# Conformer convolution in a decoder trunk: the order in which eight normed tiles go through ScalarE and VectorE

## The chip, the cores and the metric

The kernel runs on one core of one Trainium2 chip. The metric is the time of one execution on the device in microseconds; of the kernel before there are three runs, and their median stands for it. One more execution was taken with the hardware profiler, and all durations of single instructions come from that one. The engines are called by the names of the profile: PE is TensorE, which multiplies matrices (PEld is its loading of weights), DVE is VectorE, ACT is ScalarE, POOL is GpSimd, SP is SyncE, whose queue issues most transfers.

## What is computed

The reference is a trunk of two layers on 512 tokens of width 1024 in float32. Each layer is a gated feed-forward part (`ffn1`), a mixer, a second one (`ffn2`) and a gated embedding (`ple`). The mixer of layer 0 is a Conformer convolution, that of layer 1 is sparse attention. The change lies in the convolution; cut to what matters:

```python
def conformer_conv(h, w_pw1, b_pw1, w_dw, b_dw, ln_g, ln_b, w_pw2, b_pw2):
    u = h @ w_pw1 + b_pw1
    a, g = jnp.split(u, 2, axis=-1)
    u = a * jax.nn.sigmoid(g)
    u = depthwise_causal_conv(u, w_dw) + b_dw            # 31 taps
    mu = jnp.mean(u, axis=-1, keepdims=True)
    var = jnp.mean(jnp.square(u - mu), axis=-1, keepdims=True)
    u = (u - mu) * lax.rsqrt(var + LN_EPS) * ln_g + ln_b
    u = jax.nn.silu(u)
    return u @ w_pw2 + b_pw2
```

## The kernel before

Activations lie transposed: eight tiles of 128 channels by 512 tokens. To keep float32 precision every product is made of three matmuls (`mm3`): each operand is split into a rounded high part `h` and a low part `l = x - h`, and the product is `wh*h` (L420), `wh*l` (L421) and `wl*h` (L422), summed in a PSUM bank. Weights arrive by DMA as units of 128 x 1024 (`raw`), are rounded on ACT (L334, `wh`), and their low part is made on DVE or POOL (L338, `wl`); for `conv_w_pw2` it is POOL. Five such pairs of buffers are there (`HLB`), so a unit can be rounded when the unit five before it has been used up. There are eight PSUM banks.

The convolution's last part goes as follows. When the depthwise filter's eight outputs `Y[c]` are there, with a first guess of the mean already taken off, PE forms the rest of the mean (`off`, in a bank) and the token sums; from these come the inverse deviation `r` (POOL, L501) and, by PE transposes (L526), the tile `R` of it, which stays in a PSUM bank. Meanwhile PE goes through the rest of the `fill`: products of the `ple` input (`z_tiles`, operands `zp`), one bank for each tile; ACT evicts each bank into a tile `t` (L762) and SP stores it to `z` in memory (L763). This fill covers the time in which the norm is worked out.

Then, for each of the eight tiles:

```python
nc.vector.tensor_tensor(Y[c], Y[c], off, op=OP.subtract)                  # L1038, DVE
nc.vector.tensor_tensor(Y[c], Y[c], R, op=OP.mult)                        # L1039, DVE
nc.scalar.activation(Y[c], Y[c], AF.Silu, scale=ln_g, bias=ln_b)          # L1040, ACT
nc.scalar.activation(h, Y[c], AF.Copy)                                    # L1041, ACT: rounding
nc.vector.tensor_tensor(l, Y[c], h.bitcast(F32), op=OP.subtract)          # L1042, DVE: low part
```

`h` and `l` are halves of a tile called `tw` (the buffers held the filter's taps before). They are the moving operands of the product with `conv_w_pw2`: for the first four output tiles PE goes tile by tile (`k` outside, four outputs `m` inside, 12 matmuls a tile), then for the other four output by output; 192 matmuls in all.

The text of the program doesn't fix the order in which an engine runs its instructions. A planner does so when the program is built (`schedule_with_timeline_sim=True`): it goes through a simulated time and gives each engine, of the instructions that are ready, the one of highest priority, which is the one that comes first in the text. `tc.high_priority(FIN_PRI)` raises the priority of a block. `tc.issue_after(x)` puts the block's instructions behind `x` where they are on the same engine. The order so found is then fixed, each engine runs its list in that order, and semaphores hold an instruction whose operands aren't there yet.

Of the kernel before, what the change touches and what calls it, by code (L numbers as in the profile page):

```python
# [11 lines left out]
F32 = mybir.dt.float32  # L12
F32R = mybir.dt.float32r
I32 = mybir.dt.int32
AF = mybir.ActivationFunctionType
OP = mybir.AluOpType
# [13 lines left out]
FIN_PRI = 100  # L30
CALM = ("ple_w_gate", "conv_w_pw2")
FIN_AT = (1, 3)
LATE, OUT_POOL, OUT_AMID = 3, ((), (1, 3, 6)), 3
PH, LAGS = 4, 9
CONV_ON = ("pool", "dve", "dve", "pe", "pe", "pe", "pe", "pe")
# [31 lines left out]
def plan():  # L67
# [87 lines left out]
    for i in range(L):  # L155
        ffn(1, i)
        if i == 0:
            conv(0)
        else:
            nsa()  # L160
        ffn(2, i)
        full("ple_w_gate", i, KD, range(KD))
# [50 lines left out]
class Kern:  # L213
# [726 lines left out]
    def conv(self, nxt):  # L940

        nc = self.nc
        X, U, Y = self.X, {}, []
# [86 lines left out]
        R = self.spread_raw(r)  # L1030
        for _ in fill:
            pass
        V = []
        for c in range(KD):
            pair = self.ptile("tw", TWB, 128 * LAGS, F32R)
            h, l = pair[:, :512], pair[:, 512:1024]
            with self.tc.issue_after(ui if c < CENTRED else vi):
                nc.vector.tensor_tensor(Y[c], Y[c], off, op=OP.subtract)  # L1038
            nc.vector.tensor_tensor(Y[c], Y[c], R, op=OP.mult)  # L1039
            nc.scalar.activation(Y[c], Y[c], AF.Silu, scale=self.col("conv_ln_g", c), bias=self.col("conv_ln_b", c))  # L1040
            nc.scalar.activation(h, Y[c], AF.Copy)  # L1041
            nc.vector.tensor_tensor(l, Y[c], h.bitcast(F32), op=OP.subtract)  # L1042
            V.append((h, l))
        self.prep_start(*nxt)
        for ms in (range(0, 4), range(4, 8)):
            P = {m: self.bank() for m in ms}
            for k, m in [(k, m) for k in range(KD) for m in ms] if ms[0] == 0 else [(k, m) for m in ms for k in range(KD)]:
                self.mm3(P[m], self.block(("conv_w_pw2", 0, k, m)), V[k], k == 0, k == KD - 1)
                if k == KD - 1:
# [86 lines left out]
    def put_v(self, g):  # L1136
        nc, t = self.nc, self.vt
        p = self.bank()
        for kt in range(4):
            nc.tensor.transpose(p[:, kt * 128:kt * 128 + 128], t[:, kt * 128:kt * 128 + 128], self.ident)  # L1140
        V = self.Vs[g % 2]
        p8 = p.rearrange("p (i d) -> p i d", d=64)
        nc.scalar.activation(V[:, :, :64], p8, AF.Copy)
        nc.vector.tensor_tensor(V[:, :, 64:], p8, V[:, :, :64].bitcast(F32), op=OP.subtract)

# [519 lines left out]
```

## Time and profile before

| | |
|---|---|
| median of three runs | 1967.86 us (1967.64 to 1968.73) |
| the profiled execution | 1969.18 us |
| its span | 1967.4 us, 32520 instructions |
| busy: PE, DVE, ACT, POOL | 1949.2, 1539.0, 1091.4, 328.8 us |
| the eight tiles' instructions in the span | L1038 from 490.7 us, L1042 until 512.4 us |
| the 192 matmuls of `conv_w_pw2` | 500.4 to 544.3 us |

In the profile a line such as "500.41 0.69 DVE L1042 ... x1" has the start in us from the span's start, the duration, the engine and line, the operation, output and inputs with their shapes, and how many equal instructions are merged. Behind it in brackets stands how long the engine had been idle and what released it. Matmuls overlap: one starts before the one ahead has ended, so start to start is their cost.

### The profile page before, as it was taken

How to read it: one execution, taken by the hardware profiler on the slowest of the kernel's cores; microseconds unless marked ns; L12 is line 12 of the kernel's file. 1: busy time of each engine (PE TensorE's matmuls, PEld its weight loads, DVE VectorE, ACT ScalarE, POOL GpSimd, SP SyncE). 2: the span in 40 equal slices, each digit the busy share in tenths (PEclk: the TensorE clock that was granted, in tenths of full speed). 3: DMA queues.
4: the chain of work that ended last, by engine and by line, in shares of the span. 5: the costliest groups of instructions: out<-in, count | busy, mean ns of one | idle time of the engine just before them, and what ended most of it. 6: DMA issues, size and time to landing. Idle time of an engine off the chain costs nothing.

```text
span 1967.4 us, 32520 instructions
## 1 busy us (share of the span) xinstructions
PE 1949.2 (99%) x12456; PEld 1752.0 (89%) x12456; DVE 1539.0 (78%) x2708; ACT 1091.4 (55%) x1958; POOL 328.8 (17%) x362
## 2 busy tenths in 40 slices
PE   9999999999999999999999999999999999999998
PEld 7989898889889898988999989888888789998987
DVE  7879787694697796877987868636889897786875
ACT  7536356653565363546644626337888765363543
POOL 0000000442200000021000000557666300000022
PEclk9999999999999999999999999999999999999999
DMA  5323323466335343343232423463323123232241
GB/s 174 129 86 110 127 87 103 178 216 222 114 118 162 96 158 112 100 150 107 85 132 85 134 82 101 154 193 108 96 87 102 44 97 119 97 119 97 97 150 54
DMA packets 79627, 235.16 MB, mean 120 GB/s; under 512 B 8864, under 2 KB 16176, under 8 KB 79472
## 3 DMA queue, kind: packets, MB, share of 16 engines
q1 hardware_dynamic: 78512, 230.69, 35.6%
q8 instruction: 98, 1.61, 0.3%
q0 software_dynamic: 816, 2.33, 0.3%
q14 instruction: 57, 0.47, 0.1%
q10 hardware_dynamic: 144, 0.07, 0.0%
HBM read 214.66 MB, written 16.29 MB: 117 GB/s over the span
## 4 chain that ended last, share of the span: by engine, by line
PE 93%; DVE 4%; ACT 2%; issue 1%; DMA 1%; SPq 0%; POOL 0%; POOLq 0%; DVEq 0%; ACTq 0%
PE b L420 28%; PE b L421 28%; PE b L422 28%; PE b L930 2%; PE b L1289 1%; PE b L1356 1%; PE b L1375 1%; PE b L1376 1%; PE b L1228 1%; PE b L520 0%; DVE t L1359 0%; DVE s L478 0%; DMA s<-in_xT 0%; ACT s L477 0%; DVE acc L495 0%
## 5 line engine op out<-in xcount | busy, mean ns | idle before, releaser
L420 PE MATMUL b<-s,wh 128*128 128x256 f32 (+1 forms) x1416 | 445.3, 317 | 2.2 <-ACT wh L334 2.1
L421 PE MATMUL b<-s,wh 128*128 128x256 f32 (+1 forms) x1416 | 445.2, 315 | 0.5 <-DVE s L478 0.3
L422 PE MATMUL b<-s,wl 128*128 128x256 f32 (+1 forms) x1416 | 443.3, 315 | 0.0
L334 ACT ACTIVATE wh<-raw 128x1024 fp32r<-128x1024 f32 (+2 forms) x254 | 266.1, 1050 | 232.0 <-PE b L421 134.6
L420 PE MATMUL b<-px,wh 128*128 128x256 f32 (+1 forms) x1088 | 312.6, 288 | 0.5 <-ACT G L578 0.5
L421 PE MATMUL b<-px,wh 128*128 128x256 f32 (+1 forms) x1088 | 312.9, 288 | 0.0
L422 PE MATMUL b<-px,wl 128*128 128x256 f32 (+1 forms) x1088 | 312.1, 288 | 0.0
L338 DVE TENSOR_TENSOR wl<-raw,wh 128x1024 fp32r<-128x1024 f32 (+1 forms) x208 | 253.8, 1222 | 61.7 <-ACT wh L334 61.3
L420 PEld LDWEIGHTS b<-s,wh 128*128 128x128 f32 x1416 | 266.0, 188 | 21.8 <-ACT wh L334 2.7
L421 PEld LDWEIGHTS b<-s,wh 128*128 128x128 f32 x1416 | 266.0, 188 | 19.2 <-DVE s L478 0.8
L422 PEld LDWEIGHTS b<-s,wl 128*128 128x128 f32 x1416 | 264.7, 188 | 19.1 <-DVE wl L338 0.5
L421 PE MATMUL b<-hid,wh 128*128 128x512 f32 x704 | 272.7, 389 | 0.0
L422 PE MATMUL b<-hid,wl 128*128 128x512 f32 x704 | 272.6, 389 | 0.0
L420 PE MATMUL b<-hid,wh 128*128 128x512 f32 x704 | 269.4, 389 | 0.0
L338 POOL TENSOR_TENSOR wl<-raw,wh 128x1024 fp32r<-128x1024 f32 (+1 forms) x53 | 129.2, 2444 | 691.7 <-ACT wh L334 686.5
L578 ACT ACTIVATE G<-b 128x256 f32<-128x256 f32 x390 | 140.6, 378 | 130.3 <-PE b L422 104.7
L420 PEld LDWEIGHTS b<-px,wh 128*128 128x128 f32 x1088 | 204.5, 188 | 5.5 <-ACT G L578 0.8
L421 PEld LDWEIGHTS b<-px,wh 128*128 128x128 f32 x1088 | 204.8, 188 | 4.3
L422 PEld LDWEIGHTS b<-px,wl 128*128 128x128 f32 x1088 | 204.5, 188 | 3.9
L422 PEld LDWEIGHTS b<-hid,wl 128*128 128x128 f32 x704 | 132.2, 188 | 27.1
L421 PEld LDWEIGHTS b<-hid,wh 128*128 128x128 f32 x704 | 132.2, 188 | 26.9
L420 PEld LDWEIGHTS b<-hid,wh 128*128 128x128 f32 x704 | 132.2, 188 | 26.9
(251 smaller groups left out, 3582.6 us busy)
## 6 DMA issues: line engine op xcount, KB each, us to landing
raw<-in_w SPq DMA_DIRECT2D x256, 512.0 KB, 3.3
rawx<-in_w SPq DMA_DIRECT2D x78, 512.0 KB, 3.3
tw<-in_tw SPq DMA_DIRECT2D x20, 576.0 KB, 6.5
skew<-table SPq DMA_DIRECT2D x16, 320.0 KB, 5.7
z<-t SPq DMA_DIRECT2D x16, 256.0 KB, 2.6
hid<-z SPq DMA_DIRECT2D x16, 256.0 KB, 4.4
tt<-skew SPq DMA_DIRECT2D x16, 256.0 KB, 3.3
wr<-in_w SPq DMA_DIRECT2D x8, 512.0 KB, 3.6
```

The lines of the kernel that those rows point to most:

```text
L334: self.rounded = nc.scalar.activation(h[:, c], t[:, c], AF.Copy).ins
L338: eng.tensor_tensor(l[:, c], t[:, c], h[:, c].bitcast(F32), op=OP.subtract)
L420: mm(out, sh, mh, start=start, stop=False, **how)
L421: mm(out, sh, ml, start=False, stop=False, **how)
L422: self.lastmm = mm(out, sl, mh, start=False, stop=stop, **how).ins
L578: copy = lambda o, x: nc.scalar.activation(o, x, AF.Copy)
L930: nc.tensor.matmul(p[:, q * SP:q * SP + SP], T[q][:, d * 128:d * 128 + 128], u[:, q, o:o + SP], start=d == 0, stop=d == LAGS - 1)
L1228: nc.tensor.matmul(P[mh][:, :124], w, B[kk // 4][:, kk % 4, :], start=kk == 0, stop=kk == 15)
L1289: nc.tensor.matmul(p[:, :32 - lo + nk], Q, KT[:, i, "sw".index(b), lo:32 + nk], start=i == 0, stop=i == 1)
L1356: nc.tensor.transpose(p[:, a * 128:a * 128 + 128], J[a, b][:, kt * 128:kt * 128 + 128], self.ident)
L1375: nc.tensor.matmul(O, st, h, start=first, stop=False)
L1376: nc.tensor.matmul(O, st, l, start=False, stop=last)
```

## The change

The subtraction stays as it is. The first three tiles (`AHEAD`) get high priority for the four instructions behind it. On ACT each Silu goes behind the rounding of the tile before, so that the activations go tile by tile; on DVE the multiplication of tile `c`, from the fourth on, goes behind the low part of tile `c - 3`.

```diff
+AHEAD = 3
...
-        V = []
+        V, high, low = [], [], []
         for c in range(KD):
             pair = self.ptile("tw", TWB, 128 * LAGS, F32R)
             h, l = pair[:, :512], pair[:, 512:1024]
             with self.tc.issue_after(ui if c < CENTRED else vi):
                 nc.vector.tensor_tensor(Y[c], Y[c], off, op=OP.subtract)
-            nc.vector.tensor_tensor(Y[c], Y[c], R, op=OP.mult)
-            nc.scalar.activation(Y[c], Y[c], AF.Silu, scale=self.col("conv_ln_g", c), bias=self.col("conv_ln_b", c))
-            nc.scalar.activation(h, Y[c], AF.Copy)
-            nc.vector.tensor_tensor(l, Y[c], h.bitcast(F32), op=OP.subtract)
+            with self.tc.high_priority(FIN_PRI) if c < AHEAD else nullcontext():
+                with self.tc.issue_after(low[c - AHEAD]) if c >= AHEAD else nullcontext():
+                    nc.vector.tensor_tensor(Y[c], Y[c], R, op=OP.mult)
+                with self.tc.issue_after(high[c - 1]) if c else nullcontext():
+                    nc.scalar.activation(Y[c], Y[c], AF.Silu, scale=self.col("conv_ln_g", c), bias=self.col("conv_ln_b", c))
+                high.append(nc.scalar.activation(h, Y[c], AF.Copy).ins)
+                low.append(nc.vector.tensor_tensor(l, Y[c], h.bitcast(F32), op=OP.subtract).ins)
             V.append((h, l))
```

## The prediction

> **What bounds the kernel now.** I read the page first, then the windows by stage, then the waits of the stretch that the change touches, and then that stretch instruction by instruction on each engine.
>
> ```profile
> span 1967.4 us, 32520 instructions
> ...
> PE 1949.2 (99%) x12456; PEld 1752.0 (89%) x12456; DVE 1539.0 (78%) x2708; ACT 1091.4 (55%) x1958; POOL 328.8 (17%) x362
> ...
> PE 93%; DVE 4%; ACT 2%; issue 1%; DMA 1%; SPq 0%; POOL 0%; POOLq 0%; DVEq 0%; ACTq 0%
> ```
>
> TensorE (PE) is busy for 1949.2 of 1967.4 us. All that any reordering of other engines' work can win is in the 18.2 us in which it isn't. The windows say where these lie (columns: length, then busy time and instructions of PE, PEld, DVE, ACT, POOL, then the granted clock, the DMA share and GB/s):
>
> ```profile
> core 0: us, PE busy (x) PEld busy (x) DVE busy (x) ACT busy (x) POOL busy (x), PEclk, DMA share, GB/s
> 495.00:500.00 5.00, 4.35 (x21) 3.27 (x18) 5.00 (x10) 3.77 (x7) 1.80 (x1) 1.00 0.74 239
> 500.00:545.00 45.00, 44.57 (x194) 36.17 (x195) 27.79 (x34) 23.28 (x35) 10.15 (x5) 1.00 0.26 89
> ...
> 545.00:750.00 205.00, 205.00 (x1498) 192.52 (x1497) 171.81 (x247) 113.66 (x183) 1.41 (x1) 1.00 0.41 133
> 750.00:970.00 220.00, 220.00 (x1335) 196.10 (x1334) 174.62 (x252) 113.61 (x174) 21.34 (x9) 1.00 0.32 107
> ...
> 1250.00:1620.00 370.00, 364.23 (x1991) 307.90 (x1991) 285.29 (x946) 259.86 (x703) 197.79 (x272) 1.00 0.34 107
> ```
>
> In the convolution's last part, 495 to 545, PE lacks 0.65 + 0.43 = 1.08 us. From 545 to 970 it lacks nothing, and attention (1250 to 1620) lacks 5.77. The waits from 495 to 520 name what the 1.08 us is:
>
> ```profile
> DVE tw L1042 <- ACT tw L1041: 4.4, 4, 2.0
> PEld b L420 <- ACT tw L1041: 1.5, 1, 1.5
> ...
> PE b L420 <- ACT tw L1041: 1.1, 1, 1.1
> ```
>
> PE waits here once, for the first rounded tile (L1041 writes `tw`). Its timeline shows the place, between the last matmul of the ple fill and the first of `conv_w_pw2`:
>
> ```profile
> 498.96 0.39 PE L422 MATMUL b<-zp,wl 128*128 128x512 f32 x1
> 500.43 0.96 PE L420 MATMUL b<-tw,wh 128*128 128x512 f32 x3 [1.08 <-ACT tw L1041]
> ```
>
> The matmuls that follow, and their operand tiles' own instructions, from the views by tile and by line:
>
> ```profile
> L420 PE MATMUL b<-tw,wh x64: 389/389/499, 500.4 to 543.4; 128*128 128x512 f32 x64
> L422 PE MATMUL b<-tw,wl x64: 388/389/395, 501.7 to 543.9; 128*128 128x512 f32 x64
> ...
> L1040 ACT ACTIVATE y<-y,small x8: 802/804/808, 497.2 to 505.6; 128x512 f32<-128x512 f32 x8
> L1041 ACT ACTIVATE tw<-y x8: 617/619/624, 499.8 to 509.3; 128x512 fp32r<-128x512 f32 x8
> L1042 DVE TENSOR_TENSOR tw<-y,tw x8: 685/692/2468, 500.4 to 510.0; 128x512 fp32r<-128x512 f32 x8
> ```
>
> The 192 matmuls start from 500.43 to 543.9: one per 43.47 / 191 = 0.2276 us. Without a wait the first would have started one step behind 498.96, at 499.19. So the wait costs 500.43 - 499.19 = **1.24 us** of PE time, and that is all this stage has to give. Why the first tile is late stands in the timelines of ACT and DVE:
>
> ```profile
> 494.22 1.22 ACT L762 ACTIVATE t<-b 128x512 f32<-128x512 f32 x2
> 496.67 0.60 ACT L762 ACTIVATE t<-b 128x512 f32<-128x512 f32 x1 [1.23 <-PE b L422]
> 497.16 2.21 ACT L1040 ACTIVATE y<-y,small 128x512 f32<-128x512 f32 x3
> 499.28 0.57 ACT L762 ACTIVATE t<-b 128x512 f32<-128x512 f32 x1
> 499.76 0.62 ACT L1041 ACTIVATE tw<-y 128x512 fp32r<-128x512 f32 x1
> ...
> 501.50 1.05 ACT L334 ACTIVATE wh<-raw 128x1024 fp32r<-128x1024 f32 x1
> ...
> 503.16 0.58 ACT L762 ACTIVATE t<-b 128x512 f32<-128x512 f32 x1
> ...
> 506.28 2.19 ACT L1041 ACTIVATE tw<-y 128x512 fp32r<-128x512 f32 x4
> ```
>
> ```profile
> 495.52 4.87 DVE L1039 TENSOR_TENSOR y<-y,b 128x512 f32<-128x512 f32 x8
> 500.41 0.69 DVE L1042 TENSOR_TENSOR tw<-y,tw 128x512 fp32r<-128x512 f32 x1
> ...
> 504.29 1.30 DVE L1042 TENSOR_TENSOR tw<-y,tw 128x512 fp32r<-128x512 f32 x1 [1.96 <-ACT tw L1041]
> ...
> 509.96 2.47 DVE L1042 TENSOR_TENSOR tw<-y,tw 128x512 fp32r<-128x512 f32 x1 [0.53 <-ACT tw L1041]
> ```
>
> ACT runs three Silus (2.21 us) and an eviction (0.57 us) before the one rounding that PE waits for; DVE runs eight multiplications (4.87 us) before the first low part.
>
> **The change part by part.** No instruction is added or removed, and no DMA: eight multiplications, Silus, roundings and low parts stay, in another order. The subtractions (L1038) stay ahead.
>
> *The first rounding.* Multiplication 0 starts at 495.52 and takes 0.68 (4.87 less seven steps of 0.60), to 496.20. Early case: Silu 0 follows at once, 496.24 to 497.04. Late case: it stays behind the eviction of 496.67 and starts at 497.16 as now, to 497.96. Then the rounding, at once. A Silu followed by an instruction that reads its tile is not in this trace on ACT. Below, it costs nothing over the overlap of free neighbours (three Silus in 2.21: a step of 0.70, overlap 0.10). Above, it costs what this pair costs on DVE, a running sum that reads its own result:
>
> ```profile
> 479.77 1.49 DVE L917 TENSOR_TENSOR sum<-sum,t 128x512 f32<-128x512 f32 x2 [2.23 <-ACT t L916]
> ```
>
> 1.49 less the second's 0.69 is a step of 0.80, against 0.60 in L1039: 0.20 more. I take 0.15, nearer the upper end, since the row has the same dependence. So the Silu's step is 0.70 to 0.90, I say 0.85, and rounding 0 ends at 497.7 early, 498.65 late. Both are before 499.19. The first matmul then needs nothing more: **-1.24 us**. At the lower edge, the late case plus a low part (0.03 behind the rounding, 0.69 long) gives 499.37, 0.18 late only if the second matmul is the one with the low part; today matmuls of the high part alone (L420) go first, as the row of 500.43 shows. I keep 0 to 0.2 as a loss, and take 0.
>
> *The other tiles.* One tile on ACT now takes 0.85 + 0.52 (rounding's step: 2.19 for four) = 1.37, up to 0.90 + 0.62 = 1.52; I take 1.45. DVE needs 0.60 + 0.69 = 1.29 a tile, less than ACT, so low part c - 3 is normally done before multiplication c is due. PE takes 12 matmuls a tile, 12 x 0.2276 = 2.73. Tile k is wanted at 499.19 + 2.73 k: 501.92, 504.65 ... 518.30. It is there, late case, at 498.65 + 1.45 k plus what ACT has beside: two evictions (0.57, 0.58) and one L334 (1.05), 2.2 together. Tile 1: 500.10, or 501.72 with an eviction and the L334 ahead: fits by 0.2. Tile 7: 508.8 + 2.2 = 511.0: fits by 7. Cost **0**; the cover is PE's slower pace.
>
> *What is pushed back.* High priority for three tiles puts up to 3 x 1.45 = 4.35 us of ACT work ahead of evictions and of the weight rounding L334. That L334 (501.50) rounds the fifth unit of `conv_w_pw2`, wanted when 96 matmuls are done, at 499.19 + 21.85 = 521.0; even at 505, with its low part on POOL, it is 13 us early. The evictions free PSUM banks (rivals) and feed `z`, which only the ple stage behind the second ffn reads. SP issues the `z` stores and the weight loads in one queue; a later eviction holds the next load, and the next unit has the same 13 us. POOL and its queue keep their instructions. Cost **0**.
>
> *Two SBUF readers.* The low parts of 504.29 and 509.96 took 1.30 and 2.47 where the median is 0.692, while POOL ran:
>
> ```profile
> 502.63 2.41 POOL L338 TENSOR_TENSOR wl<-raw,wh 128x1024 fp32r<-128x1024 f32 x1 [5.83 <-ACT wh L334]
> 509.48 2.39 POOL L338 TENSOR_TENSOR wl<-raw,wh 128x1024 fp32r<-128x1024 f32 x1 [4.44 <-ACT wh L334]
> ```
>
> They ended at 505.59 and 512.43, each 0.55 behind POOL's end (505.04, 511.87). A low part that meets an L338 on POOL so waits for its end, up to 2.47 - 0.69 = 1.78. After the change the next multiplications wait behind it. POOL's L338 needs the L334 before it, and that needs the buffer which the fill frees at 499.19, so POOL starts at 500.3 at the earliest. Low part 0 (498.65 at the latest) is clear; low part 2 or later has room; low part 1 is the one in question (rivals). In the sum: 0. [...]
>
> *Sum.* The profiled execution took 1969.18 us around a span of 1967.4, 1.32 over the median of 1967.86 (runs from 1967.64 to 1968.73). 1969.18 - 1.24 = 1967.94; on the median 1967.86 - 1.24 = **1966.6 us**, -0.06%. A difference of about 0.2% (3.9 us) is what a measurement of this kernel can tell from none.
>
> **The rivals.**
>
> *Nothing is gained.* The planner, which fixes each engine's order when the program is built, keeps the last fill tile's eviction ahead of rounding 0. That eviction can't start before PE's 498.96 + 0.39 = 499.35, so the rounding would end at 499.35 + 0.57 + 0.62 = 500.5: 500.43 again. For it: such an eviction stands there today (499.28). Against: high priority, and Silu 0 is ready three us before. 1967.9.
>
> *An eviction comes too late (slower).* Eight banks: at 499.19 four outputs, R (held until multiplication 7) and the last three fill tiles make exactly eight. If the fourth output gets the bank of the tile evicted at 496.67 and that eviction goes behind three tiles' chain, it ends at 496.24 + 4.35 + 0.6 = 501.2 to 497.16 + 4.35 + 0.6 = 502.1. The fourth output's first matmul is due at 499.19 + 3 x 0.2276 = 499.87: PE waits 1.3 to 2.2, net 0.1 to 1.0 slower: 1968.4. It decides from an end of 501.1 on. Against: two banks were freed by 495.44 (row of 494.22), the subtraction's `off` by 495.5, the sums' bank before.
>
> *Low part 1 meets POOL.* With an eviction and the L334 ahead, low part 1 starts near 500.7, just behind an L338 that ends about 503.0, and ends at 503.5. With four high-part matmuls first, PE wants it at 501.92 + 4 x 0.2276 = 502.83: 0.7 lost, 1967.3.
>
> *The planner orders later stages anew.* Priorities and a simulated time decide the order, and the simulated time moves. Attention holds 5.77 us of PE waits: all gone is 1960.8, doubled is 1972.4. Against: 425 us without a PE gap (545 to 970) lie between, and a common shift changes no order.
>
> **How the numbers follow.** Forecast 0.57, nothing gained 0.11, late bank 0.06, low part 1 0.05, new order later 0.21 (0.07 faster by over 0.2%, 0.08 slower, 0.06 within). Same: 0.57 + 0.11 + 0.06 + 0.05 + 0.06 = 0.85; faster 0.07; slower 0.08. The forecast alone would be 1966.1 to 1967.3 (0.2 lost, runs' scatter). The range goes up to the late bank's end, 1967.86 + 1.0 = 1968.9, and down by a third of attention's 5.77: 1966.6 - 1.9 = 1964.7.
>
> **What would show it.** ACT's timeline alternating L1040 and L1041 forms from 496.2 or 497.2, the first rounding done before 498.7; PE's first `tw` matmul 0.23 behind the last `zp` one and no wait for `tw`; DVE with three multiplications ahead of the first low part; the windows from 545 on the same, 1.2 earlier. I am wrong if PE waits there for an eviction, a low part or the same rounding, or if attention's 5.77 changes by more than 1.

## The result: slower by half a per cent, and the profile after

The changed kernel takes 1978.3 us (median of six runs, 1977.02 to 1979.4), the kernel before beside it 1968.01 (1967.64 to 1968.73): a ratio of 1.0051 with a 95% interval of 1.0038 to 1.0064. The forecast of 1966.6 and its range up to 1968.9 were missed by some 10 us, on the slow side. The profiled execution took 1978.41 us around a span of 1976.6, against 1969.18 and 1967.4 before. Lines of the changed kernel stand one further down than before, from the convolution's tiles on up to four.

The page and the windows of the changed kernel, the latter in the columns shown before:

```profile
span 1976.6 us, 32527 instructions
...
PE 1951.7 (99%) x12456; PEld 1754.4 (89%) x12456; DVE 1541.3 (78%) x2708; ACT 1093.0 (55%) x1958; POOL 339.4 (17%) x362
...
PE 90%; DVE 5%; ACT 2%; DMA 1%; issue 1%; POOL 1%; SPq 0%; POOLq 0%; DVEq 0%; ACTq 0%
```

```profile
495.00:500.00 5.00, 5.00 (x25) 3.99 (x23) 3.22 (x7) 3.71 (x7) 1.90 (x1) 1.00 0.78 237
500.00:545.00 45.00, 45.00 (x198) 36.32 (x197) 31.10 (x37) 25.06 (x37) 10.15 (x5) 1.00 0.28 91
545.00:750.00 205.00, 197.60 (x1438) 185.53 (x1437) 165.28 (x237) 109.22 (x177) 12.18 (x1) 0.98 0.39 125
...
970.00:1000.00 30.00, 28.69 (x250) 28.29 (x248) 28.83 (x44) 18.38 (x32) 0.00 (x0) 1.00 0.28 91
...
1250.00:1620.00 370.00, 364.06 (x1951) 306.15 (x1950) 285.71 (x940) 257.87 (x699) 203.69 (x278) 1.00 0.35 111
```

Where the change was made, PE now lacks nothing: 5.00 of 5.00 and 45.00 of 45.00. Attention lacks 5.94 us, as good as the 5.77 before. But 545 to 750, where PE had been busy throughout, lacks 7.40 us and has a granted clock of 0.98, and POOL, with one instruction there as before, is busy for 12.18 us instead of 1.41. That is the beginning of `ffn2` of layer 0. The view of L502, the inverse root formed as a power on POOL (below "the power"), has the same instruction:

```profile
L502 POOL TENSOR_TENSOR r<-v,power x9: 695/1027/12177, 355.1 to 1968.3; 128x4 f32<-128x4 f32 x7, 128x2 f32<-128x2 f32 x2
```

Its median of nine is 1.03 us and its longest 12.18; before, the longest was 1.95. PE transposes its result (L527) and waits for it, as the waits from 545 to 580 and PE's timeline of the changed kernel say:

```profile
PE b L527 <- POOL r L502: 7.4, 1, 7.4
```

```profile
566.24 1.12 PE L527 MATMUL b<-ident,r 128*128 128x128 f32 x4 [7.40 <-POOL r L502]
567.01 0.78 PE L423 MATMUL b<-s,wl 128*128 128x512 f32 x1
567.58 0.63 PE L421 MATMUL b<-s,wh 128*128 128x512 f32 x1
568.01 0.63 PE L422 MATMUL b<-s,wh 128*128 128x512 f32 x1
...
571.01 0.39 PE L421 MATMUL b<-s,wh 128*128 128x512 f32 x1
571.24 0.40 PE L422 MATMUL b<-s,wh 128*128 128x512 f32 x1
```

In the kernel before, the same transposes followed PE's other work without a wait:

```profile
562.31 0.60 PE L526 MATMUL b<-ident,r 128*128 128x128 f32 x4
```

Behind the wait of the changed kernel a matmul follows the one ahead after 0.43 us, until about 570.5, then after 0.23 again; the windows give the granted clock there as 0.50:

```profile
566.00:567.30 1.30, 1.06 (x5) 1.06 (x6) 0.00 (x0) 0.00 (x0) 0.19 (x1) 0.50 0.00 0
567.30:570.40 3.10, 3.10 (x9) 2.43 (x8) 1.03 (x2) 0.60 (x1) 0.00 (x0) 0.50 0.02 5
570.40:573.00 2.60, 2.60 (x12) 2.11 (x12) 1.10 (x3) 1.33 (x2) 0.00 (x0) 0.98 0.00 0
```

So the stall costs more than its length: 7.4 us of waiting and some 2 us at half the clock (the transposes 1.12 for four instead of 0.60, and eight steps of 0.43 or more instead of 0.23). In this trace the clock is 0.50 from 563.7 to 570.5: it fell 4.8 us after PE had gone idle and came back 4.3 us after PE went on. In the nine profiles below with a power of 7.7 us and more it fell 2.0 to 5.1 us after PE went idle (2.0 in "3 later") and came back 3.0 to 6.1 us after PE went on, so the second price isn't a fixed one.

Counted by the n-th matmul of both traces, PE is 1.24 us earlier than before at 504, then loses 9.7 by 571, and 0.95 more near 983, where it waits for a weight rounding that waits for its DMA (28.69 of 30.00 above; before, 29.53). Of each of these losses about 0.3 comes back later. At the end it is 9.1 us behind; the span grew by 9.2.

**Why the power is so long** is to be read beside VectorE. POOL and DVE of the changed kernel from `v`, the power's input, on:

```profile
554.01 12.18 POOL L502 TENSOR_TENSOR r<-v,power 128x4 f32<-128x4 f32 x1 [14.80 <-DVE v L543]
```

```profile
553.77 0.15 DVE L543 TENSOR_SCALAR v<-b 128x4 f32<-128x4 f32 x1
553.84 0.68 DVE L567 TENSOR_TENSOR px<-t,px 128x512 fp32r<-128x512 f32 x1
554.44 0.68 DVE L364 TENSOR_TENSOR sq<-rawx,raw 128x512 f32<-128x512 f32 x1
555.04 0.68 DVE L384 TENSOR_TENSOR sq<-raw,rawx 128x512 f32<-128x512 f32 x1
...
564.00 0.69 DVE L364 TENSOR_TENSOR sq<-rawx,raw 128x512 f32<-128x512 f32 x1
564.60 0.69 DVE L394 TENSOR_TENSOR s1hl<-rawx,s1hl 128x512 fp32r<-128x512 f32 x1
568.02 0.70 DVE L703 TENSOR_TENSOR b<-b,R 128x512 f32<-128x512 f32 x1 [2.73 <-ACT R L534]
```

(`px`, `sq`, `rawx`, `s1hl`, `t` and `wl` are tiles of `ffn2`'s operands and weights.) The power starts on time. From 553.84 to 565.29 DVE runs 18 instructions that each have two inputs in SBUF (two tiles, or two halves of one), without a pause: each starts about 0.08 us before the one ahead has ended. The power ends at 566.19, 0.89 us behind the end of this run. The run ends there because DVE itself comes to the first instruction that needs the power's result: `b<-b,R` waits for `R`, which ACT makes from PE's transposes of `r`. In all nine profiles with a long power it is this instruction that ends the run. So the power is held for as long as DVE has work that doesn't depend on it. The same place of the kernel before:

```profile
556.60 1.41 POOL L501 TENSOR_TENSOR r<-v,power 128x4 f32<-128x4 f32 x1 [16.25 <-DVE v L542]
```

```profile
556.43 0.68 DVE L566 TENSOR_TENSOR px<-t,px 128x512 fp32r<-128x512 f32 x1
557.03 0.69 DVE L384 TENSOR_TENSOR rawx<-rawx 128x512 f32<-128x512 f32 x1
557.64 0.68 DVE L566 TENSOR_TENSOR px<-t,px 128x512 fp32r<-128x512 f32 x1
```

Here it ends at 558.01, 0.90 us behind the end of the first such instruction (557.11), although the next ones follow without a pause as well. An undisturbed power takes 1.01 to 1.06; the convolution's own, at 492, took 1.03 beside subtractions on DVE that follow each other as closely but have one of their inputs in PSUM. So in both kernels the power ends 0.89 to 0.90 us behind the end of a DVE instruction with two SBUF inputs: before, of the first, where it gave way to the second (the first border); after, of the last, and at none of the 17 borders ahead of it. Below, "let in at a border" means just this, a power that ends about 0.9 us behind it. The traces show when the power ends, not what holds it until then.

In order of start, by operation, tiles and shapes, the first 546 of DVE's 2708 instructions are the same in both traces, and 142 places behind them differ; PE's order differs in 507 of 12456 places, POOL's in none. Around `v` DVE had px, then the in-place sum of `rawx`, then px behind it; now it has px and two squares `sq`. (The constraints that put one instruction behind another make this whole difference: built with the priority alone, the program has the lists of the kernel before.)

### The profile page after: what moved, and what is told of

It is laid out like the page before. It is cut to its first block, busy times and chain, and to the rows that moved or that the text cites. A ratio compares the mean times of both kernels' runs of the same rounds, so it can differ in the third digit from the quotient of the medians.

```text
span 1976.6 us, 32527 instructions
## 1 busy us (share of the span) xinstructions
PE 1951.7 (99%) x12456; PEld 1754.4 (89%) x12456; DVE 1541.3 (78%) x2708; ACT 1093.0 (55%) x1958; POOL 339.4 (17%) x362
## 4 chain that ended last, share of the span: by engine, by line
PE 90%; DVE 5%; ACT 2%; DMA 1%; issue 1%; POOL 1%; SPq 0%; POOLq 0%; DVEq 0%; ACTq 0%
PE b L421 27%; PE b L422 27%; PE b L423 27%; PE b L931 2%; PE b L1293 1%; PE b L1360 1%; PE b L1379 1%; PE b L1380 1%; PE b L1232 1%; DMA raw<-in_w 1%; POOL r L502 1%; DVE t L558 0%; DVE t L1363 0%; PE b L521 0%; DVE s L479 0%
```

## The experiments

The author's theory: **exclusion** ("lock" in the expectations). A POOL power and a DVE instruction with two SBUF inputs shut each other out, as the power of 12.18 us above has it one way and the low parts beside POOL's `wl` the other (before, 1.30 and 2.47 us instead of 0.69, each ended 0.55 behind POOL's end), and where POOL misses the first border it is held to the end of DVE's run. Rivals: POOL is slow for a reason of its own; the power's delay isn't what costs the time; something else in the changed order does; and, for the first border, several ideas that came up one by one. Times of before are those of runs on the same chip.

### Without POOL: the root on VectorE

```diff
-        fin = self.rfin(self.acc, steps=first)
+        fin = self.rfin(self.acc, steps=first or i == 0)
```

> The changed kernel, but the inverse root at the start of ffn2 of layer 0 is formed on DVE by Newton steps, so that no POOL instruction stands there. Theory 'lock' (the power on POOL waited 11 us for DVE's run of instructions with two SBUF inputs, and PE for it): the stall of 7.6 us and the half clock behind it (2.2 us) go, 1978.3 - 9.8 = 1968.5 or, if the 0.95 us at 981 goes too, 1967.5; PE may wait some us for the Newton chain, which stands among other DVE work. Rival 'POOL itself' (the power is slow for a reason within POOL): the same, 1968. Rival 'order' (the new order of ffn2's DVE work costs by itself): above 1975.

Measured: 1979.87 us (1979.87 to 1979.93), ratio 1.0057 (1.0042 to 1.0072). The theory's time was missed, and the time alone would fit the rival 'order'. POOL has nothing to do there any more, but the Newton steps stand among DVE's other work, from 555.73 to 569.95, and PE waits for the last one:

```profile
PE b L527 <- DVE r L514: 9.3, 1, 9.3
```

So this run separates nothing; it shows that PE's cover is short (it began to wait 4.8 us behind the power's start, 566.24 - 7.40 - 554.01), and that PE waits for `r` whatever makes it late.

### One instruction that doesn't read SBUF, in the run

In the changed kernel, and the same in the kernel before as a control, a DVE instruction from PSUM to PSUM (128x384) is put behind `v`; the planner sets it five places further on.

```diff
             self.vins = self.nc.vector.tensor_scalar(v, p, 1e-6, None, op0=OP.add).ins
+            for n in range(gap):                 # 1 in ffn2 of layer 0
+                with self.tc.issue_after(self.vins):
+                    self.vins = self.nc.vector.tensor_scalar(b[:, 128:512], p (broadcast to 384), 1e-6, None, op0=OP.add).ins
```

> The changed kernel with one DVE instruction more in that place, which reads PSUM and writes PSUM (128x384, no SBUF operand); it stands as the sixth instruction behind v (after px, sq, sq, t, which have two SBUF inputs). [...] 'POOL itself': 12.2 us and 1978 as before. 'Order': power may be short, but the time stays above 1975.

> The changed kernel with the one PSUM instruction behind v again, in more rounds: what is left of the change when the power isn't held up. By the prediction's sum, -1.24 us of PE wait in the convolution: 1966.6 to 1968 where the kernel before takes 1968 to 1969; ratio 0.9994, with an interval that may reach 1. If the new order costs something by itself: at or above the kernel before.

> The kernel before with the same PSUM instruction added (sixth behind v). Its power takes 1.41 us without it. 'Lock': the power stays at 1.4, the convolution's wait of 1.24 us stays, time as the kernel before within 0.5 us; so what e2 wins over it is the convolution's. If the added instruction wins something by itself: below the kernel before by 1 us or more.

Measured, changed kernel: 1968.3 (1966.92 to 1968.94), ratio 0.9997 (0.9988 to 1.0007), and on another chip 1969.07, 0.9999 (0.9991 to 1.0008); kernel before: 1968.94, 0.9997 (0.9989 to 1.0006). POOL and DVE of the first:

```profile
552.99 2.95 POOL L502 TENSOR_TENSOR r<-v,power 128x4 f32<-128x4 f32 x1 [14.86 <-DVE v L544]
```

```profile
552.82 0.68 DVE L571 TENSOR_TENSOR px<-t,px 128x512 fp32r<-128x512 f32 x1
553.42 0.68 DVE L364 TENSOR_TENSOR sq<-rawx,raw 128x512 f32<-128x512 f32 x1
554.02 0.68 DVE L384 TENSOR_TENSOR sq<-raw,rawx 128x512 f32<-128x512 f32 x1
554.62 0.42 DVE L562 TENSOR_TENSOR t<-G,t 128x256 f32<-128x256 f32 x1
554.96 0.56 DVE L547 TENSOR_SCALAR b<-b 128x384 f32<-128x384 f32 x1
```

The power ends at 555.94, 0.9 behind the end of the fourth instruction (555.04), when the one without SBUF inputs has begun, and not at the run's end: as exclusion has it, with the 0.89 us of the changed kernel (555.04 + 0.89 = 555.93). PE doesn't wait, and the 10 us are gone. Up to the power's end DVE's order is that of the changed kernel with one instruction more; only behind it do some 40 others stand elsewhere. So the loss is the power's delay, and DVE's run is what delays it; POOL has the same instruction in both, so it isn't slow by itself.

### The kind of the second instruction

The kernel before had the in-place sum where the changed one has the square; in this one the square goes behind the second in-place sum.

```diff
-            nc.vector.tensor_tensor(q[:, lo], u[:, lo], t[:, lo], op=OP.subtract)
+            with self.tc.issue_after(self.added_up) if self.now == ("ffn2", 0) else nullcontext():
+                nc.vector.tensor_tensor(q[:, lo], u[:, lo], t[:, lo], op=OP.subtract)
...
-        nc.vector.tensor_tensor(u[:, lo], u[:, lo], u[:, hi], op=OP.add)
+        self.added_up = nc.vector.tensor_tensor(u[:, lo], u[:, lo], u[:, hi], op=OP.add).ins
```

> The changed kernel with one DVE instruction moved: the second weight difference (sq from rawx and raw) goes behind the second in-place sum (rawx from rawx), eighth instead of second behind v. DVE still goes without a break from one instruction with two SBUF inputs to the next. 'Lock held over a run': the power again takes 11 to 12 us, 1977 to 1979. 'Lock, but the kind of the next instruction decides at each border': the power ends 0.9 us behind some border earlier than the end of the run, 2 to 7 us. 'POOL itself': 12.2 us, 1978.

Measured: 1979.61 (1978.95 to 1979.83), ratio 1.0055 (1.004 to 1.007); the power took 12.52 us and ended 0.90 behind the run's end. The other square (L384 of the changed kernel) came second instead, so it tells little of the kind; it is one more run in which no border let POOL in.

### Runs of added instructions, in other places of the kernel before

Behind `v` in places where DVE was idle: first eight sums that write PSUM (with two SBUF inputs or one), then sums of two tiles into SBUF (`hid<-s,s`).

```diff
+            for kind in probe:                   # 8 in ple of layer 0, 3 in ffn2 of layer 1, 8 in ple of layer 1
+                o = self.ptile("hid", HIDS)
+                with self.tc.issue_after(self.vins):
+                    self.nc.vector.tensor_tensor(o, self.xs[0], self.xs[1], op=OP.add)
```

> The kernel before, with eight DVE instructions added directly behind v in three places where DVE is otherwise idle and the power on POOL took 1.02 to 1.06 us: at ple of layer 0 eight sums of two SBUF tiles (384 columns, about 0.47 us apart), at the start of attention eight sums of two halves of one SBUF tile (256 columns, 0.33 apart), at ple of layer 1 eight sums of an SBUF tile and a PSUM bank (384). 'Lock held over a run': 8 x 0.47 + 0.9 = 4.7 us in the first, 8 x 0.33 + 0.9 = 3.6 in the second, 1.0 in the third. 'Lock given at the next border': 0.5 + 0.9 = 1.4, 1.3 and 1.0. 'POOL itself': 1.0 in all three.

> The kernel before with DVE instructions of two SBUF inputs added behind v where DVE is otherwise idle, this time each with an output of its own, so that they run without the pause of 35 ns that the first probe had between them: eight sums of two tiles (512 columns, 0.60 us apart) at ple of layer 0; three ahead of the wl at ffn2 of layer 1; at ple of layer 1 a sum of two tiles, one of two halves of a tile, and six of two tiles. 'Lock held over a run': power about 8 x 0.60 - 0.17 + 0.9 = 5.5 us in the first place, 3 x 0.6 + 1.1 + 0.9 = 3.8 or more in the second, 5.2 in the third. 'Lock given at the next border': 0.5 + 0.9 = 1.4 in all three.

Measured: with PSUM outputs, powers of 1.26, 1.07 and 1.01 us; these instructions had pauses of 35 ns between them. With SBUF outputs, without pauses, 1.39, 1.41 and 1.38: POOL came in at the first border in all three, where exclusion over a whole run would have given 5.5, 3.8 and 5.2 by the expectation. Times 1970.38 and 1972.63 (single executions, with the added work). So a run without pauses isn't enough: something decides at the first border. The power of 1.95 us at `ffn2` of layer 1 (near 1583), behind a `wl` of 1024 and ahead of two more such instructions without a pause, says the same: it was let in at the first border in the kernel before, in the changed one and in every other run that left its place as it was (1.94 to 1.95).

### AHEAD = 1

```diff
-AHEAD = 3
+AHEAD = 1
```

> The changed kernel with AHEAD = 1: on DVE each multiplication waits for the low part just ahead. The order of DVE at ffn2 differs again: behind v come the in-place sum (rawx from rawx), px, sq, t, s1hl, sq, wl, px and on, 14 instructions with two SBUF inputs, about 10 us. 'Lock held over a run': power 10 to 11 us; PE's transposes stand later here (as in the kernel before), so its wait is 4 to 6 us with some half clock behind: 1972 to 1975. 'A border with the in-place sum lets POOL in' (as in the kernel before, where it stands second): power 1.4 to 2.0, 1967 to 1968.

> AHEAD = 1 once more, for a profile of one of its slow executions. If the profiled execution is near 1978 to 1980, the power at ffn2 of layer 0 takes 10 to 12.5 us there, ends 0.87 to 0.90 us behind the end of VectorE's run of two-SBUF-input instructions, and PE waits 5 to 8 us for it; if it is near 1968 to 1971, the power takes 1.4 us again, with the same order of instructions.

> AHEAD = 1 a third time, for a profile of one of its slow executions: if it is near 1978 to 1980, the power at ffn2 of layer 0 takes 10 to 12.5 us and PE waits 5 to 8 us for it there; if near 1968 to 1971, the power takes 1.4 us.

Measured: 1978.66 median over 12 executions, ratio 1.0032 (1.0018 to 1.0046), but these are of two kinds, which the ratio mixes: four from 1967.94 to 1971.45 and eight from 1978.18 to 1980.37, longer than either forecast. All three profiled executions fell among the quick ones (1971.45, 1968.1 and 1966.92), with powers of 1.41 us let in at the first border. That the slow ones hold a long power at the same place is inferred from their size; no profile shows one. If so, the list of instructions alone doesn't decide the first border: one program goes either way.

### Small instructions ahead of the run: one, two, five

The changed kernel with small DVE instructions (128x4, from PSUM, 0.07 us start to start) directly behind `v`. With one, it is the only difference in DVE's order; with two and five, some others move, but only behind 560.

```diff
+            for n in range(gap):                 # 1, 2 or 5 in ffn2 of layer 0
+                with self.tc.issue_after(self.vins):
+                    j = self.tiny.tile([128, 4], F32, name="j", tag=("vj", "ra", "u")[n // 2])
+                    self.vins = self.nc.vector.tensor_scalar(j, p, 1e-6, None, op0=OP.add).ins
```

> The changed kernel with one small VectorE instruction (128x4, PSUM in, some 0.07 us) directly behind v of ffn2 of layer 0; the run of instructions with two SBUF inputs and everything else keep their order, only their start against the power on POOL moves by about 0.07 us. Theory 'a close race at the first border': the power may now be let in behind the first of them (1.4 to 1.5 us, time 1967.5 to 1969.5) or still miss it (12 us, 1977.5 to 1980). Rival 'the kind of the second instruction decides (the square where before had the in-place sum)': the order of kinds is the changed kernel's, so 12 us and 1977.5 to 1980 here and with two small ones.

> As the run with one, but two small VectorE instructions behind v, so the run of two-SBUF-input instructions starts some 0.14 us later against the power. Race: if 0.07 us was not enough to let POOL in, 0.14 may be; a time near 1968 with a power of 1.4 to 1.5 us, or near 1978.5 with 12 us; mixed results among the executions would speak for a race of a few ns. Kind of the second instruction: 12 us and 1977.5 to 1980.

> As the run with one, but five small VectorE instructions behind v, so that the first two-SBUF-input instruction starts 0.3 us later, behind the power's own start of reading (some 0.13 us behind v's end). [...] Rival 'something else in the changed order makes the power slow': it stays at 12 us and 1977.5 to 1980.

Measured: one, 1977.06 (1976.01 to 1977.83), ratio 1.0037 (1.0023 to 1.0052), power 12.25; two, 1977.88 (1976.46 to 1978.17), 1.004 (1.0025 to 1.0055), power 12.32; five, 1967.71 (1965.86 to 1969.27), 0.9991 (0.9982 to 1.0). A shift of the run by 0.07 or 0.14 us against the power changes nothing: a close race for the first border is not supported. With five, the run starts 0.17 us behind the power:

```profile
552.91 1.03 POOL L502 TENSOR_TENSOR r<-v,power 128x4 f32<-128x4 f32 x1 [14.56 <-DVE v L543]
```

```profile
552.67 0.15 DVE L543 TENSOR_SCALAR v<-b 128x4 f32<-128x4 f32 x1
552.74 0.42 DVE L547 TENSOR_SCALAR j<-b 128x4 f32<-128x4 f32 x5
553.08 0.68 DVE L571 TENSOR_TENSOR px<-t,px 128x512 fp32r<-128x512 f32 x1
```

POOL has gone first, the power takes its undisturbed 1.03, and DVE's first instruction isn't longer for it (0.68). The expectation's 0.13 us from the end of `v` to the power's reading is the author's estimate: the power's row begins 0.09 us behind that end (552.82), and no row shows a reading. This is the change without its loss, and what it is worth is 1.3 us between the medians (0 to 3.5 by the interval), no more than a measurement of this kernel can tell from none: in the profiled execution, of the 1.24 won at 499 the wait near 977 (1.16 by PE's start times) takes most back here too.

### The changed kernel's pair in the kernel before

```diff
-            self.vins = self.nc.vector.tensor_scalar(v, p, 1e-6, None, op0=OP.add).ins
+            with self.tc.issue_after(self.added_up) if self.now == ("ffn2", 0) else nullcontext():
+                self.vins = self.nc.vector.tensor_scalar(v, p, 1e-6, None, op0=OP.add).ins
```

> The kernel before, with v of ffn2 of layer 0 held two places back on VectorE (behind the second in-place sum): behind v stand px and then the square sq, the pair that the changed kernel has there, all else as before. Theory 'the pair at the first border decides': the power misses it and takes 8 to 13 us, 1976 to 1980. Rival 'the convolution's new order decides through something else': the power takes 1.4 us and the time is 1967.5 to 1969.5.

Measured: 1977.97 (1976.71 to 1978.29), ratio 1.0043 (1.0027 to 1.0058). POOL, DVE and the waits of this run; the kernel is the one before, with `v` two places later and the order ahead of it unchanged:

```profile
557.28 11.50 POOL L501 TENSOR_TENSOR r<-v,power 128x4 f32<-128x4 f32 x1 [17.50 <-DVE v L543]
```

```profile
557.11 0.68 DVE L567 TENSOR_TENSOR px<-t,px 128x512 fp32r<-128x512 f32 x1
557.71 0.68 DVE L363 TENSOR_TENSOR sq<-rawx,raw 128x512 f32<-128x512 f32 x1
...
567.47 0.41 DVE L558 TENSOR_TENSOR t<-G,t 128x256 f32<-128x256 f32 x1
```

```profile
PE b L526 <- POOL r L501: 6.5, 1, 6.5
```

The power ends at 568.78, 0.90 behind the run's end (567.88), with the convolution as it was. The loss thus needs nothing of the change itself: the place of `v` in DVE's list is enough.

### Other pairs at the first border of the changed kernel

`v` later by three or nine places; then a list in which the in-place sum stands at the first border, as in all profiles of this place in which POOL was let in there; then the instruction of the probes above.

```diff
+            with self.tc.issue_after(self.differed) if self.now == ("ffn2", 0) else nullcontext():   # 3 later
+            with self.tc.issue_after(self.added_up) if self.now == ("ffn2", 0) else nullcontext():   # 9 later
                 self.vins = self.nc.vector.tensor_scalar(v, p, 1e-6, None, op0=OP.add).ins
...
+            with self.tc.issue_after(self.lowed) if ...:                   # in place: v behind s1hl,
                 self.vins = ...
+            with self.tc.issue_after(self.added_up) if ...:                # and px and t behind the in-place sum
...
+            for _ in range(probe):                                         # own three, directly behind v
+                o = self.ptile("hid", HIDS)
+                with self.tc.issue_after(self.vins):
+                    self.vins = self.nc.vector.tensor_tensor(o, self.xs[0], self.xs[1], op=OP.add).ins
```

> The changed kernel with v of ffn2 of layer 0 three places later on VectorE (behind the second difference of sq): behind v stand t (128x256) and then s1hl. 'The pair decides': another pair, so the power may be let in at once, 1.1 to 1.4 us and 1967.5 to 1970 (v itself comes 1.8 us later, still under PE's cover). 'Something else in the changed order': missed again, 9 to 11 us and 1976 to 1980.

> The changed kernel with v nine places later on VectorE (behind the second in-place sum): behind v stand the sum into rawx (L366) and the low part wl of 1024. v comes some 5 us later, which uses up most of PE's cover (PE began to wait 4.8 us behind the power's start). 'The pair decides': let in at the first border, a power of 1.4 us, PE waits 1 to 3 us, 1968 to 1972. 'Something else': missed until the end of VectorE's run, 6 to 8 us of power, PE waits 7 to 9 us, 1977 to 1981.

> The changed kernel with five VectorE instructions of ffn2 of layer 0 reordered: v stands behind s1hl, and behind v stand t (128x512) and then the in-place sum of rawx. In every profile in which the power was let in at the first border of this place, the in-place sum stood at that border; in none of those that missed it. Theory 'the instructions at the border decide' (an in-place sum lets POOL in): 1.4 us of power, 1967.5 to 1971. Rival 'what stands at the border doesn't decide': missed, 8 to 11 us of power, 1974 to 1980.

> The changed kernel with three added sums of two tiles in SBUF (128x512, the instruction of p2_probe, which let POOL in at the first border each time) directly behind v, then VectorE's run as before them. 'The instructions at the border decide': let in behind the first of the three, 1.4 us, time 1967.5 to 1972 (1.8 us more VectorE work). 'What stands at the border doesn't decide': 12 to 15 us of power, 1977 to 1983.

Measured:

| | us (lowest to highest) | ratio (95%) | power, us | behind the run's end |
|---|---|---|---|---|
| 3 later | 1975.99 (1973.58 to 1977.92) | 1.0034 (1.0021 to 1.0047) | 10.71 | 0.90 |
| 9 later | 1975.32 (1974.12 to 1978.06) | 1.0033 (1.0019 to 1.0047) | 7.70 | 0.90 |
| in place | 1974.48 (1973.91 to 1975.39) | 1.0034 (1.0021 to 1.0047) | 9.77 | 0.90 |
| own three | 1976.91 (1975.07 to 1979.36) | 1.0045 (1.0029 to 1.0061) | 11.24 | 0.90 |

All four missed the first border and every later one. POOL and DVE of the last two, the first with the in-place sum as second instruction, as in the kernel before, the second with the probes' pair:

```profile
556.57 9.77 POOL L505 TENSOR_TENSOR r<-v,power 128x4 f32<-128x4 f32 x1 [17.41 <-DVE v L547]
```

```profile
556.39 0.68 DVE L562 TENSOR_TENSOR t<-G 128x512 f32<-128x512 f32 x1
556.99 0.69 DVE L385 TENSOR_TENSOR rawx<-rawx 128x512 f32<-128x512 f32 x1
```

```profile
552.86 11.24 POOL L502 TENSOR_TENSOR r<-v,power 128x4 f32<-128x4 f32 x1 [14.78 <-DVE v L543]
```

```profile
552.68 1.89 DVE L547 TENSOR_TENSOR hid<-s,s 128x512 f32<-128x512 f32 x3
```

So the idea that the instructions at the first border decide falls too. **What decides it stays open.** What was found: it isn't the kinds of the two instructions there alone, nor a shift of 0.07 or 0.14 us, nor the convolution's order. The traces hold a lead that doesn't settle it: between `v` and the second instruction of the run, DVE's queue has a semaphore wait of its own (no busy time, so not in the rows above) in nine of the eleven profiles of this place that missed the first border and in one of the seven that were let in; "3 later" and "9 later" missed without one, and the kernel before with the PSUM instruction was let in with one. What remains is all or nothing: in every profile of this place in which DVE's run had begun first, POOL came in at the first border or, until an instruction without two SBUF inputs or a pause came, at none.

## Why the prediction was wrong, step by step

- **The first rounding, -1.24 us: right.** PE's and ACT's timelines of the changed kernel:

```profile
499.06 0.39 PE L423 MATMUL b<-zp,wl 128*128 128x512 f32 x1
499.30 1.20 PE L421 MATMUL b<-tw,wh 128*128 128x512 f32 x4
```

```profile
497.26 0.80 ACT L1044 ACTIVATE y<-y,small 128x512 f32<-128x512 f32 x1
498.12 0.60 ACT L763 ACTIVATE t<-b 128x512 f32<-128x512 f32 x1
498.62 0.62 ACT L1045 ACTIVATE tw<-y 128x512 fp32r<-128x512 f32 x1
...
501.79 0.81 ACT L1044 ACTIVATE y<-y,small 128x512 f32<-128x512 f32 x1
502.63 0.63 ACT L1045 ACTIVATE tw<-y 128x512 fp32r<-128x512 f32 x1
```

  The first `tw` matmul follows the last `zp` one by 0.24 with no wait. It was closer than forecast: an eviction still stands between Silu 0 and rounding 0, which ended at 499.24 instead of 498.65. A Silu with its dependent rounding directly behind takes a step of 0.84; 0.85 was taken.
- **The other tiles and what is pushed back, cost 0: right in the stage.** PE is busy for 45.00 of 45.00 us; the weight rounding came at 499.85 instead of 501.50, not later. Behind the stage it was wrong (next point).
- **The step that failed: "POOL and its queue keep their instructions. Cost **0**", with "Two SBUF readers" weighed in one place only.** The low part's wait for POOL's `wl` came where it was looked for: two low parts of the changed kernel took 1.99 and 2.48 us, each ended 0.55 behind POOL's end (503.37 and 510.17), and they cost PE nothing, as said. But the exclusion was weighed for the eight tiles alone. The one POOL instruction whose result PE needs with little cover, the power at 554, was put at nothing because POOL keeps its instructions. It does keep them, but this one took 12.18 us instead of 1.41, and PE waited 7.4 for it and lost 9.7 in all. What had kept it short was that POOL was let in at the first border; why it isn't in the new order is open. The rows of before had the sign of it: one power in nine at 1.41 and one at 1.95 where the median is 1.03.
- **"The planner orders later stages anew": the rival that came true, with the wrong place and size.** Its argument against itself failed: 425 us without a PE gap do not keep the order. 142 places of DVE's order changed, most of them between 550 and 675, and the gap opened there, at 559. It was sized by attention's 5.77 us, which stayed (5.94), so its slow case was 1972.4 at most, and the range, taken from another rival, ended at 1968.9.
- **The stall's second price, some 2 us at the half clock, was in no case of the prediction.** In the kernel before PE has no gap from 545 to 970 and a granted clock of 1.00 there; its trace has the half clock in attention, though, 0.50 for 3.4 us from 1605.4 on.
- **The other rivals** did not occur: something was gained, no eviction came late, low part 1 cost nothing.

## What to carry to other kernels

Where a planner makes the order, a small edit is a new order for everything behind it: look for short instructions with little cover on the path that sets the end, and ask what their neighbours on other engines might become, before calling a later stage unchanged. A short POOL instruction with SBUF operands whose result TensorE needs soon is one to look at where it starts beside a long run of VectorE instructions with two SBUF inputs: here it took 12.18 us beside a run of 18, and 0.34 us of small PSUM-sourced instructions between its input and the run took that down to 1.03. A busy engine's slack is to be judged by the wait plus a slower clock behind it: here 7.4 us of waiting, with a granted clock of 0.50 until 4.3 us after it, cost 9.7.

## What the hardware showed that was not expected

- A power of 128x4 on POOL, 1.01 to 1.06 us by itself, took 7.7 to 12.5 us beside VectorE runs of two-SBUF-input instructions, and ended 0.89 to 0.90 us behind the last of them each time. In the changed kernel it waited over 17 borders between instructions and not for one, while in the kernel before and at three added places one border was enough (1.38 to 1.41 us).
- VectorE isn't slowed when POOL gets in: behind the border that let it in, the in-place sum took 0.69 us, as elsewhere. The power's last 0.90 us (557.11 to 558.01) lay beside that sum and the px behind it (0.68).
- One program (AHEAD = 1) ran in 1968 to 1971 us in four executions of twelve and in 1978 to 1980 in the other eight.
